# Attention heads of a hybrid decoder layer as one pipeline of branches beside the projection units

## The chip, the cores and the metric

The kernel runs on one core of one Trainium2 chip. The metric is the time of one execution on the device in microseconds (us). The engines are called PE (matmuls; PEld is its weight loading), DVE (vector), ACT (scalar), POOL (GpSimd) and SP (which issues most DMAs). On-chip memory has 128 partitions; matmul results go to eight PSUM buffers, which are handed out here under the tags "g", "s", "t" (two each), "m" and "o" (one each).

## The reference

One layer with 512 tokens and width 2048, all in float32:

```python
h = _rms_norm(x, attn_norm)
proj = h @ w_in     # 8 FoX heads q,k,v + forget gates; 8 NSA heads q; 2 KV groups x (kc,vc,ks,vs,kw,vw); gates
# FoX head:  softmax(q k^T * scale + cum_f[query] - cum_f[key], causal) @ v      (q, k RMS-normed)
# NSA head:  gate0 * compressed + gate1 * selected + gate2 * window attention    (ALiBi slopes, q, k RMS-normed)
#   compressed keys/values: 31 blocks of 32 tokens through cmp_w_k, cmp_w_v
x = x + concat(fox, nsa) @ w_out
h = _rms_norm(x, ffn_norm)
x = x + (silu(h @ w_gate) * (h @ w_up)) @ w_down
```

With 512 tokens the selected branch takes all 8 blocks and the window covers all earlier tokens, so both are causal attention over the full length with their own keys and values.

## The kernel before

Everything is computed transposed, 128 rows of width by 512 tokens. Each float32 operand is split into a high and a low fp32r part (`split`: ACT writes the high part, DVE the low part), and a product is three matmuls (`mm3`: high x high, high x low, low x high).

The work comes in stages. First, `x` and the first weights are loaded and the four token products of kc and vc are formed (`first`). Then come 20 projection *units*: each takes one [2048 x 256] block of `w_in`, in four weight tiles of 1024 columns (`load_w`: a load on SP into one of three "ws" buffers, a split into one of two "wp" buffers), and accumulates 192 matmuls into two "g" buffers (`unit`, `pair_steps`). A unit of queries or keys ends with RMS norms and transposes (`normed`): ACT and DVE square, sum, invert and scale the tile `t` ("tk", one buffer), PE transposes it twice ("nT", four transposes each), and the result is split into a tile of tag "u" (four buffers). A unit of values is split straight into a "u" tile. The second unit carries also the gates (`values_and_gates`, 288 columns).

Beside the units stand the side works. `unload` and `windows` prepare the kc and vc tokens: half 0 goes into the tag "pt" (one buffer, which attention uses for its transposed probabilities), half 1 into "u". `compress` multiplies them with `cmpw` (32 matmuls each for kc and vc, into "m"). `gates` makes gates and forget sums. Then the heads: `nsa(h)` runs the scores of the selected branch (`Branch.scores`: four score tiles, each three matmuls, then DVE adds the bias and takes the row minimum, ACT exponentiates; at the end four DVE multiplies by the inverse sums), the scores of the window branch, the compressed softmax, then the transposes (`Branch.transposes`, ten small PE transposes in three "t" buffers, split into "pt") and the products with the values (`Branch.pv`) of one branch after the other into one "o" buffer. `fox(h)` is one branch, whose bias rows POOL makes from `ckb`, a broadcast load of forget sums. `keep` copies the head's output to its own tile.

All these are Python generators whose steps are interleaved by `weave(main, side, ...)`: for each step of the units, so many steps of the side work. The pairings are written out by hand: two NSA heads beside one unit (nsa_q(2), nsa_q(6)), or beside two (nsa_k(1) with vs1; fox_qk(0) with fox_v(0)); none beside nsa_q(4); two FoX heads beside three units; head 6 beside the last unit; head 7 has no unit beside it. This order is a priority only. The framework plans each engine's queue from it, and puts an instruction whose operands it expects later behind others that it expects to be ready. [...]

After the heads, their outputs are split into the 16 blocks of `bigm` (which held the normalized input until the last unit is done), and 16 output tiles `po` of 48 matmuls with 512 columns follow (`gemm_steps`), each followed by the residual add and the preparation of the feed-forward input (`x1_steps`, `form_sums`, `form_parts`). Then the gate and up stage (`q`, line 971) and the down stage (`pd`) run; the change does not touch them, but for the place of two tiles: `ca` and `cb`, in a pool that takes over the bytes of the weight buffers "ws" and "wp". The load with index 1 of the gate and up stage goes into `cb`, the one with index 4 into `ca`.

Of the kernel before, what the change touches and what calls it, by code (L numbers as in the profile page):

```python
# [16 lines left out]
P = 128  # L17
D = 2048
T = 512
# [34 lines left out]
SHIFT = 8  # L54
SKEW = 48
WSLOT = 2 * HALF * P + P

# [5 lines left out]
UNITS = 2 * NJ  # L63
NOX = 13


@with_exitstack
def hybrid_layer(ctx: ExitStack, tc: tile.TileContext, xT, vec, ffb, wfirst, wgate, win, cmpw, wout, wgu, wdn, out):
# [206 lines left out]
    def pair_steps(name, done):  # L275
# [3 lines left out]
        yield from unit(z, name, win[i], 4, 2 * P, 2 * P, lambda g: done(g, z[g]))  # L279

    def unit_tile(name):
        return ap_.tile([P, 4 * T + 16], FR, tag="u", name=name, bufs=4)

    def normed(na, nb, ga, gb):
# [12 lines left out]
        yield from pair_steps(na, done)  # L297
        nc.vector.tensor_tensor(w, w, e2[:, :, None].to_broadcast([P, NB, 2]), op=OP.add)
        nc.scalar.activation(y, w, AF.Ln, scale=1.0 / HD)
        nc.scalar.activation(y, y, AF.Exp, scale=-0.5)  # L300
        nc.vector.scalar_tensor_tensor(v, w, -0.5 / HD, y, op0=OP.mult, op1=OP.mult)
        nc.vector.tensor_tensor(v, v, y, op=OP.mult)
        nc.vector.scalar_tensor_tensor(y, v, 1.5, y, op0=OP.add, op1=OP.mult)
        nc.vector.tensor_tensor(t, t, y[:, :, :, None].to_broadcast([P, NB, 2, P]), op=OP.mult)
        yield
        r = unit_tile(na)
        for a, (name, gain) in enumerate(((na, ga), (nb, gb))):
            yield
            o = ps.tile([P, T], F32, tag="t", name=f"nT_{name}", bufs=2)
            for i in range(NB):  # L310
                nc.tensor.transpose(o[:, i * P:(i + 1) * P], t[:, i, a, :], ident)
            d = r[:, a * 2 * T:(a + 1) * 2 * T].rearrange("p (s t) -> p s t", s=2)
            split(d, o, gain)
            live[name] = d
            yield

# [10 lines left out]
    def values(na, nb):  # L327
# [9 lines left out]
        yield from pair_steps(na, done)  # L337
        yield

# [13 lines left out]
    class Branch:  # L353
# [5 lines left out]
        def scores(self):  # L359
# [3 lines left out]
            for i in reversed(range(NB)):  # L363
# [6 lines left out]
                nc.scalar.activation(pi, pi, AF.Exp, scale=-1.0, bias=st[:, 0, i:i + 1], accum_out=st[:, 1, i:i + 1])  # L370
                yield
            nc.vector.tensor_scalar_max(st[:, 2], st[:, 1], 1e-30)
# [3 lines left out]
            for i in reversed(range(NB)):  # L376
                pi = p[:, POFF[i]:POFF[i] + P * (i + 1)]
                nc.vector.tensor_scalar_mul(pi, pi, st[:, 2, i:i + 1])

        def transposes(self):  # L380
# [14 lines left out]
        def pv(self, o, start, stop):  # L395
            v, pt = self.v, self.pt
            for n, j in enumerate((0, 1, 3, 2)):
# [7 lines left out]
    def keep(h, o):  # L405
        if h == 0:
            oT[h] = ap_.tile([P, 2, T], F32, tag="fr", name=f"o{h}")[:, 0]
        elif h == NH - 2:
            oT[h] = ap_.tile([P, T], F32, tag="tk", name=f"o{h}")
# [58 lines left out]

    def compressed(h, q, o):
        g = h // 4  # L470
# [26 lines left out]
        yield  # L497
        mm3(o, Vc[:, 0], Vc[:, 1], pt[:64, 0], pt[:64, 1], False, False)
        yield
# [44 lines left out]

    def nsa(h):
        g = h // 4
        q = live.pop(f"qn{h}")
# [4 lines left out]
        o = ps.tile([P, T], F32, tag="o", name=f"on{h}")  # L552
        s, w = [Branch(f"{b}{h}", q, live[f"k{m}{g}"], live[f"v{m}{g}"],
                       lambda i: nb[:, T - P * (i + 1):], 3 * h + c)
                for b, m, c in (("s", "s", 1), ("w", "w", 2))]
        c = compressed(h, q, o)
        yield from s.scores()
        yield from w.scores()
        next(c)
        yield  # L560
        yield from s.transposes()
        next(c)
        yield
        yield from s.pv(o, True, False)
        yield from c
        yield from w.transposes()
        yield from w.pv(o, False, True)
        keep(NH + h, o)

    def fox(h):  # L570
        q, k, v = [live.pop(f"{m}f{h}") for m in "qkv"]
        ck = ap_.tile([P, T], F32, tag="ck", name=f"ckb{h}")
        nc.sync.dma_start(ck, cumd[h:h + 1, :].to_broadcast([P, T]))
        o = ps.tile([P, T], F32, tag="o", name=f"of{h}")

        def nbs(i):
            n = P * (i + 1)
            nb = ap_.tile([P, T], F32, tag="nb", name=f"nbf{h}{i}", bufs=2)
            nc.gpsimd.tensor_scalar(nb[:, :n], ck[:, :n], ncq[:, i, h:h + 1], 1.0, op0=OP.add, op1=OP.mult)  # L579
            nc.gpsimd.affine_select(nb[:, n - P:n], nb[:, n - P:n], pattern=[[-1, P]], compare_op=OP.is_ge,  # L580
                                    fill=BIG, base=0, channel_multiplier=1)
            return nb[:, :n]

        f = Branch(f"f{h}", q, k, v, nbs, None)
        yield from f.scores()
        yield from f.transposes()
        yield from f.pv(o, True, True)
        if h == NH - 1:
            oT[h] = o
        else:  # L590
            keep(h, o)

# [4 lines left out]
    def nsa_q(h):  # L597
        return normed(f"qn{h}", f"qn{h + 1}", gneg[:, 1:2], gneg[:, 1:2])

# [45 lines left out]

    N, NV, NS, FS = 38, 33, 26, 11
    weave(k0, chain(unload(), windows("kc", V_PK)), N, 9, 6)
    weave(values_and_gates("vs0", "vw0"), chain(compress("kc"), windows("vc", V_PV)), 32, 38)
    weave(nsa_q(0), chain(gates(), compress("vc")), N, 35)
    weave(nsa_q(2), chain(nsa(0), nsa(1)), N, 2 * NS)  # L650
    weave(chain(nsa_k(1), values("vs1", "vw1")), chain(nsa(2), nsa(3)), N + NV, 2 * NS)
    run(nsa_q(4))
    weave(nsa_q(6), chain(nsa(4), nsa(5)), N, 2 * NS)
    weave(chain(fox_qk(0), fox_v(0)), chain(nsa(6), nsa(7)), N + NV, 2 * NS)
    for h in range(0, NH - 2, 2):
        weave(chain(fox_qk(h + 1), fox_qk(h + 2), fox_v(h + 2)), chain(fox(h), fox(h + 1)), 2 * N + NV, 2 * FS)
    weave(fox_qk(NH - 1), fox(NH - 2), N, FS)
    last = fox(NH - 1)


    order = list(range(NH, 2 * NH)) + list(range(NH))
    om = []
    for i, h in enumerate(order[:-1]):
        t = big(i)
        split(t, oT[h])
        om.append(t)
    run(last)
    t = big(NK - 1)
    split(t, oT[NH - 1])
    om.append(t)  # L670
    att.close()
# [45 lines left out]

    for m in range(NK):
        n = m // 2 + HALF * (m % 2)
# [494 lines left out]
```

## Time and profile before

| | |
|---|---|
| median of 3 runs | 2147.38 us (2146.97 to 2147.62) |
| the profiled execution | 2147.01 us, its span 2145.3 us |
| granted TensorE clock, mean | 0.997 |
| PE busy | 2113.4 us (99%), 17023 matmuls |
| DVE busy | 1639.2 us (76%) |
| ACT busy | 956.4 us (45%) |
| POOL busy | 185.9 us (9%) |

The span is the time from the first to the last recorded instruction; the execution's own time is 1.7 us longer. Busy times are sums over an engine's instructions. A matmul's end is modelled, and consecutive matmuls overlap in the record, so PE's busy share says little about lost time; the distance from start to start says more. In the lists of waits a line reads: engine, tile and line that waited, the instruction whose result ended the wait, total us, number of waits, longest.

By the tiles' names, the first token products run from about 5 to 50 us, the units with the NSA heads from about 53 to 415, those with the FoX heads to about 710, the output tiles to 872, the gate and up stage and the down stage fill the rest.

### The profile page before, as it was taken

The numbers are of one execution on the slowest core, as the hardware profiler recorded it, in microseconds if no ns is written. First come the engines' busy times: TensorE is split into PE (matmuls) and PEld (weight loads), VectorE is DVE, ScalarE is ACT, GpSimd is POOL, SyncE is SP. The second block draws the span as 40 slices with busy tenths as digits, with TensorE's granted clock in tenths as the row PEclk, the third lists the DMA queues.
The fourth block names the chain that finished last, engine by engine and source line by source line (L and its number), as shares of the span: only waits on it lengthen the run. The fifth ranks groups of instructions, "written<-read, shape, count | busy, mean of one in ns | idle before, by whom it ended". The sixth has DMA issues, their size and how long they took to land.

```text
span 2145.3 us, 40678 instructions
## 1 busy us (share of the span) xinstructions
PE 2113.4 (99%) x17023; PEld 2047.8 (95%) x17023; DVE 1639.2 (76%) x2429; ACT 956.4 (45%) x1179; POOL 185.9 (9%) x297
## 2 busy tenths in 40 slices
PE   8989999999999999999999999999999999999998
PEld 7988999999999888899999999999999999999998
DVE  6656556544445544799999999999999987889898
ACT  5435334433345433443443434333443455565553
POOL 1000000010100000111111111111111000000000
PEclk9999999999999999999999999999999999999999
DMA  5511121132222344567677776777777797579864
GB/s 187 177 65 40 60 70 50 50 99 85 85 89 89 118 147 143 143 186 202 193 182 202 188 197 184 193 201 180 207 186 193 216 341 270 150 230 330 292 180 138
DMA packets 113353, 350.60 MB, mean 163 GB/s; under 512 B 13576, under 2 KB 13576, under 8 KB 113168
## 3 DMA queue, kind: packets, MB, share of 16 engines
q1 hardware_dynamic: 85408, 271.12, 37.6%
q0 software_dynamic: 22144, 52.44, 14.0%
q10 hardware_dynamic: 5616, 24.43, 2.9%
q8 instruction: 133, 2.18, 0.4%
q14 instruction: 52, 0.43, 0.1%
HBM read 319.35 MB, written 74.73 MB: 184 GB/s over the span
## 4 chain that ended last, share of the span: by engine, by line
PE 77%; issue 15%; DVE 3%; POOL 1%; DMA 1%; ACT 1%; ACTq 0%; POOLq 0%; SPq 0%; DVEq 0%
PE q L971 39%; PE pd L1106 13%; PE pd L1111 6%; PE po L149 3%; PE po L148 3%; PE po L147 3%; DMA ckb<-cumd 1%; PE ps_qn L267 1%; PE ps_qn L265 1%; PE ps_qn L268 1%; POOL nbf L579 1%; PE ps_first L149 1%; PE ps_first L147 1%; PE ps_first L148 1%; PE ps_ks L265 1%
## 5 line engine op out<-in xcount | busy, mean ns | idle before, releaser
L79 ACT ACTIVATE bigm<-r 128x1792 fp32r<-128x1792 f32 x174 | 298.2, 1714 | 469.1 <-PE q L971 299.5
L76 DVE TENSOR_TENSOR bigm<-r,bigm 128x1792 fp32r<-128x1792 f32 x174 | 351.5, 2020 | 11.7 <-ACT bigm L79 11.4
L76 DVE TENSOR_TENSOR r<-r 128x512 f32<-128x512 f32 x522 | 267.3, 512 | 28.9 <-DMA r<-wgu 16.8
L971 PE MATMUL q<-formx,bigm 128*128 128x256 f32 x1848 | 218.4, 277 | 2.6 <-ACT bigm L79 2.6
L971 PE MATMUL q<-bigm 128*128 128x256 f32 x1848 | 217.8, 277 | 0.0
L971 PEld LDWEIGHTS q<-formx,bigm 128*128 128x128 f32 x1848 | 214.4, 189 | 2.8 <-ACT bigm L79 2.8
L971 PE MATMUL q<-formy,bigm 128*128 128x256 f32 x1848 | 216.9, 276 | 0.0
L971 PE MATMUL q<-forma,bigm 128*128 128x256 f32 x1848 | 216.8, 276 | 0.0
L971 PEld LDWEIGHTS q<-bigm 128*128 128x128 f32 x1848 | 213.8, 188 | 0.0
L971 PEld LDWEIGHTS q<-forma,bigm 128*128 128x128 f32 x1848 | 213.1, 188 | 0.1
L971 PEld LDWEIGHTS q<-formy,bigm 128*128 128x128 f32 x1848 | 213.0, 188 | 0.1
L121 POOL DMA_DIRECT2D wsum<-wdn x176 | 119.8, 687 | 868.0 <-ACT bigm L79 764.6
L1106 PE MATMUL pd<-bigm 128*128 128x256 f32 x1224 | 147.9, 276 | 0.0
L265 PE MATMUL ps_qf<-wp_qf,bigm 128*128 128x256 f32 x512 | 144.7, 283 | 0.0
L1106 PEld LDWEIGHTS pd<-bigm 128*128 128x128 f32 x1224 | 143.0, 188 | 0.0
L268 PE MATMUL ps_qf<-wp_qf,bigm 128*128 128x256 f32 x512 | 142.7, 279 | 0.0
L267 PE MATMUL ps_qf<-wp_qf,bigm 128*128 128x256 f32 x512 | 142.3, 278 | 0.0
L76 DVE TENSOR_TENSOR bigm<-wd,bigm 128x2048 fp32r<-128x2048 f32 (+1 forms) x64 | 110.3, 1724 | 12.3 <-ACT bigm L79 12.0
L79 ACT ACTIVATE bigm<-rawm 128x768 fp32r<-128x768 f32 (+2 forms) x72 | 65.9, 924 | 109.4 <-PE pd L1111 62.9
L149 PE MATMUL po<-bigm,wp_o 128*128 128x512 f32 x256 | 99.8, 390 | 0.0
L148 PE MATMUL po<-bigm,wp_o 128*128 128x512 f32 x256 | 99.7, 389 | 0.0
L147 PE MATMUL po<-bigm,wp_o 128*128 128x512 f32 x256 | 99.6, 390 | 0.0
(415 smaller groups left out, 4458.0 us busy)
## 6 DMA issues: line engine op xcount, KB each, us to landing
r<-wgu SPq DMA_DIRECT2D x174, 512.0 KB, 4.3
wsum<-wdn POOLq DMA_DIRECT2D x176, 256.0 KB, 4.9
rawm<-ad SPq DMA_DIRECT2D x44, 512.0 KB, 6.5
wd<-wdn SPq DMA_DIRECT2D x40, 512.0 KB, 5.8
wd<-wsum SPq DMA_DIRECT2D x40, 512.0 KB, 6.9
ad<-cb ACTq DMA_DIRECT2D x22, 896.0 KB, 5.6
rawm<-ad SPq DMA_DIRECT2D x44, 384.0 KB, 3.3
ws_qf<-win SPq DMA_DIRECT2D x32, 512.0 KB, 3.2
```

The lines of the kernel that those rows point to most:

```text
L76: return pin(nc.vector.tensor_tensor(*args, op=op))
L79: return pin(nc.scalar.activation(*args, **kw))
L121: d = nc.gpsimd.dma_start(step[0], step[1], **step[2])
L147: nc.tensor.matmul(o, lh, rh, start=start, stop=False)
L148: nc.tensor.matmul(o, lh, rl, start=False, stop=False)
L149: nc.tensor.matmul(o, ll, rh, start=False, stop=stop)
L265: nc.tensor.matmul(o, xg[k][:, 0, c], wp[:, 0, w], start=(k == 0 and b == 0), stop=False, skip_group_check=True)
L267: nc.tensor.matmul(o, xg[k][:, 0, c], wp[:, 1, w], start=False, stop=False, skip_group_check=True)
L268: nc.tensor.matmul(o, xg[k][:, 1, c], wp[:, 0, w], start=False, stop=(k == NK - 1), skip_group_check=True)
L971: nc.tensor.matmul(o, w[wp][:, fb, cs], a[:, xp, fa], start=(k == 0 and h == 0 and wp == 0 and xp == 0), stop=(g == NG - 1 and kk == 1 and ...
L1106: nc.tensor.matmul(b[q][k][:, h * 256:(h + 1) * 256], w[0][:, fb, q * P:(q + 1) * P], a[xp][:, fa], start=(j == 0 and h == 0 and xp == 0), ...
L1111: nc.tensor.matmul(b[q][k][:, h * 256:(h + 1) * 256], w[1][:, fb, q * P:(q + 1) * P], a[0][:, fa], start=False, stop=(j == NJ - 1), skip_g ...
```

## The change

* `weave` now takes a list of side works, each with a first and a last step of the main work between which its steps are spread evenly.
* All units form one stream of 32 steps each (`stream`). A unit of queries or keys leaves its norm's last part behind (`finish`): the elementwise work is issued at the unit's end, the transposes of the two halves after 4 and 6 steps of the next unit.
* All heads form one list of 24 branches (`branches`: selected and window for each NSA head, one for each FoX head). `attend` interleaves the four score steps of a branch with the three transpose steps of the branch before it, and then runs that branch's products. The compressed softmax follows the selected branch's scores, its transposes the window branch's scores, its product stands within the selected branch's products.
* The bias of the next NSA head (`slopes`) and the forget row of the next FoX head (`forget_row`) are made after the first score of a head's first branch.
* 193 steps of attention are spread from step 104 to step 320 (the eight NSA heads; from unit 4 to unit 10 of 20), then 11 at a time over windows of 1.15 to 1.55 units. vc's windows stand at steps 26 to 42 instead of behind kc's products.
* The pool of 13 [128 x 512] buffers becomes 8, and a spare tile of 5 x 512 (tag "x5") that holds one after the other: the first weights in five slices, half 0 of vc's windows, the queries 0 and 1, the queries 4 and 5, the outputs of FoX heads 0 to 4.
* Eight of the 16 output splits stand in the last unit. The first two output tiles are formed together, in the order 8 + 8, 6 + 6, 2 + 2 of their 16 steps, with the last unit's norm and the last head beside them; both residual adds come after.
* Units vs1 and nsa_q(4) change places; `cb` is allocated before `ca`.

No matmul, transpose, elementwise instruction or DMA is added or left out.

```diff
-NOX = 13
+FIN = 4
+NOX = 8
...
-    def weave(main, side, n, m, d=0, r=0):
-        done = 0
-        for i, _ in enumerate(main):
-            while done * (n - d) < (i + 1 - d) * (m - r) and next(side, side) is not side:
-                done += 1
-        run(side)
+    def weave(main, sides, at=0):
+        done = [0] * len(sides)
+        for i, _ in enumerate(main, at + 1):
+            for s, (lo, hi, n, gen) in enumerate(sides):
+                while done[s] < n and i >= lo + (hi - lo) * done[s] / n:
+                    next(gen, None)
+                    done[s] += 1
...
+    def stream(units):
+        behind = iter(())
+        for steps in units:
+            for i, _ in enumerate(steps):
+                if i in (FIN, FIN + 2):
+                    next(behind, None)
+                yield
+            behind = live.pop("finish", iter(()))
+            next(behind, None)
+        live["finish"] = behind
...
             if half == 0:
-                xb = ap_.tile([P, 2, 1280], FR, tag="pt", name=f"xb_{which}").rearrange("p s c -> p (s c)")
+                xb = (ap_.tile([P, 2 * 1280], FR, tag="pt", name=f"xb_{which}") if which == "kc" else spare_unit(f"xb_{which}"))
...
+    def attend(brs):
+        def products(b):
+            if b.start:
+                live["o"] = ps.tile([P, T], F32, tag="o", name=f"o_{b.name}")
+            for n, _ in enumerate(b.pv(live["o"], b.start, b.stop)):
+                yield
+                if n == 0 and b.start and not b.stop:
+                    next(b.side)
+                    yield
+            if b.stop:
+                keep(b.head, live["o"])
+        last = None
+        for b in brs:
+            a = b.scores()
+            t = last.transposes() if last else iter(())
+            for n in range(4):
+                next(a)
+                yield
+                if n == 0:
+                    b.more()
+                if last and n < 3:
+                    next(t)
+                    yield
+            if b.head >= NH:
+                next(b.side)
+                yield
+            if last:
+                yield from products(last)
+            last = b
+        for _ in last.transposes():
+            yield
+        yield from products(last)
...
+    early = spare("early")
     for k in range(NK):
...
-        ws = oxp.tile([P, T], F32, tag="ox", name=f"w0_{k}", bufs=NOX)
+        ws = early[:, k % 5 * T:(k % 5 + 1) * T]
...
+    plan = [(2, 30, 9, chain(unload(), windows("kc", V_PK))), (26, 42, 4, windows("vc", V_PV)),
+            (34, 62, 36, compress("kc")), (66, 96, 40, chain(gates(), compress("vc")))]
+    first_score = 3 * U + FIN + 4
+    plan.append((first_score, 10 * U, 8 * 25 - 7, rest))
+    for a, b in ((10.05, 11.2), (11.25, 12.55), (12.6, 14.15), (14.25, 15.55), (15.6, 17.15), (17.25, 18.55), (18.6, 20)):
+        plan.append((a * U, b * U, 11, rest))
+    plan.append((19 * U + 17, 20 * U, 8, out_splits()))
+    weave(stream(units), plan)
...
+        for k0, k1 in ((0, 8), (8, 14), (14, 16)):
+            for m, n in enumerate((0, HALF)):
+                if k0 % HALF == 0:
+                    wp[m] = load_w(wout[n, k0 // HALF], f"o{n}_{k0 // HALF}")
+                for k in range(k0, k1):
+                    if k == len(om):
+                        out_split()
+                    c = slice(k % HALF * P, (k % HALF + 1) * P)
+                    mm3(z[m], wp[m][:, 0, c], wp[m][:, 1, c], om[k][:, 0, :], om[k][:, 1, :], k == 0, k == NK - 1)
+                    yield
+    plan = [(7, 10, 2, live.pop("finish")), (9, 27, 20, rest)]
+    weave(first_outs(), plan)
+    run(rest)
...
+    cb = fpl.tile([P, 4, T], F32, name="cb")
     ca = fpl.tile([P, 4, T], F32, name="ca")
-    cb = fpl.tile([P, 4, T], F32, name="cb")
```

More of the change, by code (lines that the diff above doesn't have):

```diff
@@ L279, in pair_steps, with spare, spare_unit, normed @@
         yield from unit(z, name, win[i], 4, 2 * P, 2 * P, lambda g: done(g, z[g]))
+    def spare(name, dtype=F32):
+        return oxp.tile([P, 5 * T], dtype, tag="x5", name=name)
+    def spare_unit(name):
+        return spare(name, FR)
     def unit_tile(name):
         return ap_.tile([P, 4 * T + 16], FR, tag="u", name=name, bufs=4)
-    def normed(na, nb, ga, gb):
+    def normed(na, nb, ga, gb, tile=unit_tile):
         t = ap_.tile([P, NB, 2, P], F32, tag="tk", name=f"t_{na}")
@@ L297, in normed @@
         yield from pair_steps(na, done)
[L298 to L304, printed above, removed]
@@ L305, in normed, with finish @@
-        yield
-        r = unit_tile(na)
-        for a, (name, gain) in enumerate(((na, ga), (nb, gb))):
-            yield
[L309 to L315, printed above, removed]
+        def finish():
+            nc.vector.tensor_tensor(w, w, e2[:, :, None].to_broadcast([P, NB, 2]), op=OP.add)
+            nc.scalar.activation(y, w, AF.Ln, scale=1.0 / HD)
+            nc.scalar.activation(y, y, AF.Exp, scale=-0.5)
+            nc.vector.scalar_tensor_tensor(v, w, -0.5 / HD, y, op0=OP.mult, op1=OP.mult)
+            nc.vector.tensor_tensor(v, v, y, op=OP.mult)
+            nc.vector.scalar_tensor_tensor(y, v, 1.5, y, op0=OP.add, op1=OP.mult)
+            nc.vector.tensor_tensor(t, t, y[:, :, :, None].to_broadcast([P, NB, 2, P]), op=OP.mult)
+            yield
+            r = tile(na)
+            for a, (name, gain) in enumerate(((na, ga), (nb, gb))):
+                o = ps.tile([P, T], F32, tag="t", name=f"nT_{name}", bufs=2)
+                for i in range(NB):
+                    nc.tensor.transpose(o[:, i * P:(i + 1) * P], t[:, i, a, :], ident)
+                d = r[:, a * 2 * T:(a + 1) * 2 * T].rearrange("p (s t) -> p s t", s=2)
+                split(d, o, gain)
+                live[name] = d
+                yield
@@ L317, in split_values @@
+        live["finish"] = finish()
+    def stream(units):
[8 more added lines that the diff above has]
+        live["finish"] = behind
     def split_values(r, i, z):
@@ L337, in values @@
         yield from pair_steps(na, done)
-        yield
     def values_and_gates(na, nb):
@@ L395, in pv @@
         def pv(self, o, start, stop):
-            v, pt = self.v, self.pt
+            v, pt = live[self.v], self.pt
             for n, j in enumerate((0, 1, 3, 2)):
@@ L405, in keep @@
     def keep(h, o):
[L406 to L409, printed above, removed]
+        if h == NH - 1:
+            oT[h] = o
+            return
+        if h < NH - 3:
+            if h == 0:
+                live["x5"] = spare("o_fox")
+            oT[h] = live["x5"][:, h * T:(h + 1) * T]
+        elif h < NH - 1:
+            oT[h] = ap_.tile([P, 2 * T], F32, tag=("fr", "tk")[h - NH + 3], name=f"o{h}")[:, :T]
         else:
@@ L467, in compress, with compressed @@
             split(Vc, r)
-    def compressed(h, q, o):
+    def compressed(h, q):
         g = h // 4
@@ L497, in compressed @@
         yield
-        mm3(o, Vc[:, 0], Vc[:, 1], pt[:64, 0], pt[:64, 1], False, False)
+        mm3(live["o"], Vc[:, 0], Vc[:, 1], pt[:64, 0], pt[:64, 1], False, False)
         yield
@@ L543, in gates, with slopes @@
         nc.vector.tensor_scalar_mul(ncq, tq, -1.0)
-    def nsa(h):
-        g = h // 4
-        q = live.pop(f"qn{h}")
+    def slopes(h):
         nb = ap_.tile([P, T], F32, tag="nb", name=f"nb{h}", bufs=2)
@@ L551, in nsa @@
         nc.gpsimd.affine_select(nb, nb, pattern=[[-1, T]], compare_op=OP.is_ge, fill=FAR, base=384, channel_multiplier=1)
[L552 to L591, printed above, removed]
@@ new lines, in slopes, with forget_row, branches, nbs @@
+        live[f"nb{h}"] = nb
+    def forget_row(h):
+        if h < NH:
+            live[f"ck{h}"] = ck = ap_.tile([P, T], F32, tag="ck", name=f"ckb{h}")
+            nc.sync.dma_start(ck, cumd[h:h + 1, :].to_broadcast([P, T]))
+    def branches(first, last):
+        for h in range(first, last):
+            if h < NH:
+                g = h // 4
+                q = live.pop(f"qn{h}")
+                if h == 0:
+                    slopes(0)
+                nb = live.pop(f"nb{h}")
+                for b, c in (("s", 1), ("w", 2)):
+                    br = Branch(f"{b}{h}", q, live[f"k{b}{g}"], f"v{b}{g}", lambda i: nb[:, T - P * (i + 1):], 3 * h + c)
+                    br.head, br.start, br.stop = NH + h, b == "s", b == "w"
+                    br.side = live[f"c{h}"] = compressed(h, q) if b == "s" else live[f"c{h}"]
+                    br.more = (lambda: slopes(h + 1)) if b == "s" and h < NH - 1 else (lambda: None)
+                    yield br
+            else:
+                f = h - NH
+                q, k = live.pop(f"qf{f}"), live.pop(f"kf{f}")
+                if f == 0:
+                    forget_row(0)
+                ck = live.pop(f"ck{f}")
+                def nbs(i):
+                    n = P * (i + 1)
+                    nb = ap_.tile([P, T], F32, tag="nb", name=f"nbf{f}{i}", bufs=2)
+                    nc.gpsimd.tensor_scalar(nb[:, :n], ck[:, :n], ncq[:, i, f:f + 1], 1.0, op0=OP.add, op1=OP.mult)
+                    nc.gpsimd.affine_select(nb[:, n - P:n], nb[:, n - P:n], pattern=[[-1, P]], compare_op=OP.is_ge,
+                                            fill=BIG, base=0, channel_multiplier=1)
+                    return nb[:, :n]
+                br = Branch(f"f{f}", q, k, f"vf{f}", nbs, None)
+                br.head, br.start, br.stop, br.side = f, True, True, iter(())
+                br.more = lambda: forget_row(f + 1)
+                yield br
@@ L644, in unload @@
                 yield
[L646 to L658, printed above, removed]
     order = list(range(NH, 2 * NH)) + list(range(NH))
     om = []
-    for i, h in enumerate(order[:-1]):
-        t = big(i)
-        split(t, oT[h])
+    def out_split():
+        t = big(len(om))
+        split(t, oT[order[len(om)]])
         om.append(t)
-    run(last)
-    t = big(NK - 1)
@@ L669, in hybrid_layer, with out_splits @@
-    split(t, oT[NH - 1])
-    om.append(t)
+    def out_splits():
+        for _ in range(8):
+            out_split()
+            yield
+    U = 32
+    units = [k0, values_and_gates("vs0", "vw0"), nsa_q(0), nsa_q(2), nsa_k(1), nsa_q(4), values("vs1", "vw1"), nsa_q(6),
+             fox_qk(0), fox_v(0)]
+    for h in range(0, NH - 2, 2):
+        units += [fox_qk(h + 1), fox_qk(h + 2), fox_v(h + 2)]
+    units.append(fox_qk(NH - 1))
+    rest = attend(branches(0, 2 * NH))
+    plan = [(2, 30, 9, chain(unload(), windows("kc", V_PK))), (26, 42, 4, windows("vc", V_PV)),
+            (34, 62, 36, compress("kc")), (66, 96, 40, chain(gates(), compress("vc")))]
@@ new lines, in hybrid_layer, with first_outs @@
+    first_score = 3 * U + FIN + 4
[4 more added lines that the diff above has]
+    weave(stream(units), plan)
+    x1steps = {}
+    z = [ps.tile([P, T], F32, tag="g", name=f"po{n}", bufs=2) for n in (0, HALF)]
+    def first_outs():
+        wp = {}
+        for k0, k1 in ((0, 8), (8, 14), (14, 16)):
[4 more added lines that the diff above has]
+                    if k == len(om):
+                        out_split()
+                    c = slice(k % HALF * P, (k % HALF + 1) * P)
+                    mm3(z[m], wp[m][:, 0, c], wp[m][:, 1, c], om[k][:, 0, :], om[k][:, 1, :], k == 0, k == NK - 1)
+                    yield
@@ L716, in x1_steps @@
             tt(acc, acc, sq, op=OP.add)
-    for m in range(NK):
+    for m in range(2):
+        x1s = x1_steps(m)
+        next(x1s)
+        live["z"] = z[m]
+        run(x1s)
+    form_sums(live["raw"])
+    form_parts(0, live["raw"])
+    for m in range(2, NK):
         n = m // 2 + HALF * (m % 2)
```

8 lines of the change are left out of this document (5 added, 3 removed).

## The prediction

> **What bounds the kernel now.** I read the page's busy times first, then the list of who waited for whom on the tensor engine, then the order of time around its longest waits.
>
> ```profile
> span 2145.3 us, 40678 instructions
> PE 2113.4 (99%) x17023; PEld 2047.8 (95%) x17023; DVE 1639.2 (76%) x2429; ACT 956.4 (45%) x1179; POOL 185.9 (9%) x297
> ```
>
> The matmul engine is busy for 99% of the span, so nothing that leaves the number of matmuls alone can bring more than the gaps between them. The change keeps every matmul, transpose, DMA and elementwise instruction and only moves them, so its worth is the waits of PE it removes, less those it makes. From 20 to 720 us (all of the mixer that is touched) PE waited for this:
>
> ```profile
> PE ps_qn L267 <- DVE wp_qn L76: 4.0, 1, 4.0
> PE nT_qf L311 <- DVE t_qf L304: 3.0, 7, 0.7
> PE pcT L494 <- DVE pc L490: 2.2, 6, 0.7
> PE pT_f L390 <- DVE p_f L378: 1.5, 2, 0.9
> PE ps_qn L265 <- ACT vs L319: 1.2, 1, 1.2
> PE pT_s L390 <- DVE pt_s L76: 1.2, 3, 0.5
> PE zkT L464 <- DVE zks L461: 0.5, 1, 0.5
> PE s_s L147 <- DVE st_s L369: 0.5, 2, 0.2
> PE pT_s L390 <- DVE p_s L378: 0.4, 2, 0.2
> PE ps_qn L265 <- DVE tf L349: 0.4, 1, 0.4
> PE nT_qn L311 <- DVE t_qn L304: 0.4, 1, 0.4
> PE nT_ks L311 <- DVE t_ks L304: 0.2, 1, 0.2
> ```
>
> Columns: total us, times, longest us. Together 15.5 us in 28 waits; nearly all end with a vector result. That is idle time as the view counts it, and it is too little, because a matmul's recorded end overlaps the next one's start:
>
> ```profile
> 256.57 0.28 PE L268 MATMUL ps_vs<-wp_vs,bigm 128*128 128x256 f32 x1
> 256.69 0.40 PE L147 MATMUL on<-pt_s,vs 128*128 128x512 f32 x1
> 257.72 0.60 PE L494 MATMUL pcT<-ident,pc 128*64 128x128 f32 x4 [0.64 <-DVE pc L490]
> 258.08 0.48 PE L148 MATMUL on<-pt_s,vs 128*128 128x512 f32 x1
> 258.39 0.39 PE L149 MATMUL on<-pt_s,vs 128*128 128x512 f32 x1
> ```
>
> A matmul of 256 columns is recorded as 0.28 us, yet the next starts 0.12 us later; one of 512 columns takes about twice that, 0.24. Here the next start comes 1.03 us after the one at 256.69, so 0.79 us is lost where the row says 0.64, and the next 512-column matmul takes 0.31 instead of 0.24. I add 0.25 us to each wait: 0.16 hidden, 0.09 to get going again.
>
> **The change part by part.**
>
> (1) The first vc window leaves the one "pt" buffer for the spare tile "x5". Now it cannot be written before the last kc product has read its own window from "pt". These rows show the pile-up that follows, ACT and DVE first, PE after:
>
> ```profile
> 105.23 0.27 ACT L453 ACTIVATE zs_kc<-z_kc 64x128 f32<-64x128 f32 x1 [2.38 <-PE z_kc L450]
> 107.87 0.62 ACT L431 ACTIVATE xb_vc<-xt_vc 128x512 fp32r<-128x512 f32 x1
> 114.12 0.68 DVE L432 TENSOR_TENSOR xb_vc<-xt_vc,xb_vc 128x512 fp32r<-128x512 f32 x1
> 114.88 1.22 DVE L76 TENSOR_TENSOR wp_qn<-ws_qn,wp_qn 128x1024 fp32r<-128x1024 f32 x1
> ```
>
> ```profile
> 108.89 0.29 PE L268 MATMUL ps_fg<-wp_fg,bigm 128*128 128x288 f32 x1
> 110.35 0.36 PE L265 MATMUL ps_qn<-wp_qn,bigm 128*128 128x256 f32 x1 [1.17 <-ACT vs L319]
> 111.85 0.35 PE L265 MATMUL ps_qn<-wp_qn,bigm 128*128 128x256 f32 x1 [0.37 <-DVE tf L349]
> 116.16 0.58 PE L267 MATMUL ps_qn<-wp_qn,bigm 128*128 128x256 f32 x1 [3.95 <-DVE wp_qn L76]
> 116.53 0.41 PE L268 MATMUL ps_qn<-wp_qn,bigm 128*128 128x256 f32 x1
> 119.31 0.41 PE L265 MATMUL ps_qn<-wp_qn,bigm 128*128 128x256 f32 x1
> ```
>
> ```profile
> 113.00:120.00 7.00, 3.85 (x16) 3.45 (x17) 6.44 (x16) 1.60 (x5) 0.61 (x1) 0.51 0.23 75
> 140.00:420.00 280.00, 274.27 (x2091) 257.17 (x2091) 169.03 (x468) 126.09 (x284) 13.52 (x22) 1.00 0.17 54
> 152.00:200.00 48.00, 46.66 (x335) 41.94 (x334) 31.89 (x103) 23.23 (x58) 4.00 (x6) 1.00 0.14 45
> 278.00:303.00 25.00, 24.85 (x216) 24.42 (x215) 8.98 (x13) 6.73 (x10) 0.00 (x0) 1.00 0.28 89
> ```
>
> DVE reaches the second half of the query weights at 114.88, behind four windows and four value evictions, all due within 8 us. From 108.89 up to the one at 119.31 PE starts 17 projection matmuls (14 of them from 116.16 on) and one small transpose. At 0.12 us each these are 2.2 us of 10.4: lost 8.2. Of that, 1.5 us is a halved clock: in the first row (busy us of PE, weight loads, DVE, ACT and POOL with counts, then granted clock, DMA share, GB/s) the granted clock is 0.51, and from 116.53 to 119.31 thirteen starts are 0.214 us apart instead of 0.114 (13 x 0.10 = 1.3, and the first pair). After the change the vc windows come in steps 26 to 42, where the spare tile is free. Their own cover is the gate unit, 32 steps of about 0.8 us. What is late next is the kc normalization chain behind zkT (0.5 us in the list). I take 7.5 us; the ends are 0 (the four value evictions alone keep DVE late) and 8.2.
>
> [...]
>
> (2) Attention as one pipeline, 193 steps spread over 216 unit steps, with the selected branch's transposes and products behind the next branch's scores. The waits that belong to the NSA heads (pcT, pT_s, s_s, nT_qn, nT_ks) are 2.2 + 1.2 + 0.5 + 0.4 + 0.4 + 0.2 = 4.9 us in 15. With 0.25 each: 8.7. Each is a softmax or norm that PE reaches too early. The compressed softmax now gets 3 transposes between it and pcT, after it 11 steps; a score's PSUM buffer gets a transpose and unit work before its next use; norms get 4 unit steps. The vector load, which is 66% in 152 to 200 us and 36% in 278 to 303, where no head runs, evens out to about 60% (169 of 280 us from 140 to 420). Ends: 0 (the vector queue is as late as now) and 14, since waits under 0.15 us are not listed: about 5 more by the same kind of restart. I take 8.7.
>
> (3) Norms and transposes of a projection pair stand in the next unit, and FoX heads use the same pipeline: nT_qf 3.0 in 7 and pT_f 1.5 in 2, with 9 x 0.25: 6.8 us. The last pT_f waits are those of heads 6 and 7, which have only little beside them now; in the new order two output tiles, 32 steps of 3 matmuls or 32 x 3 x 0.24 = 23 us, stand beside the last head. I take 6.8; ends 2 and 7.
>
> (4) The first two output tiles together make one new wait. The last four steps use the second half-matrices of both tiles: tile 0's weight slot comes free when 2 steps of tile 1 (6 x 0.24 = 1.4 us) remain, and must be split for the third tile:
>
> ```profile
> 711.59 1.06 ACT L79 ACTIVATE wp_o<-ws_o 128x1024 fp32r<-128x1024 f32 x1 [1.54 <-PE po L149]
> 712.68 1.23 DVE L76 TENSOR_TENSOR wp_o<-ws_o,wp_o 128x1024 fp32r<-128x1024 f32 x1 [0.40 <-ACT wp_o L79]
> ```
>
> From the release to the end of the second instruction 2.3 us: PE stands about 1 us, 3 at most if the two residual adds go first.
>
> (5) Costed at nothing: five "early" slices plus eight buffers for thirteen shared ones (a load has 5 x 12 x 0.24 = 14 us of matmuls to land, and the row below says 3); the splits of the first eight head outputs in the last unit, hidden by its 192 matmuls (were that cover gone, each would cost PE at most what the larger split in (4) takes, 2.3 us); the forget rows' loads on the SP queue, issued one head ahead as the buffer comes free; head outputs in "x5", free by then.
>
> ```profile
> 1.26 3.09 DMA w<-wfirst
> ```
>
> (6) The swap of ca and cb. These rows show the start of the gate and up stage:
>
> ```profile
> 872.79 0.33 SPq L82 DMA_DIRECT2D cb<-wgu  x1
> 878.57 1.70 ACT L79 ACTIVATE bigm<-cb 128x1792 fp32r<-128x1792 f32 x1 [7.62 <-DVE cb L76]
> 880.32 5.92 PE L971 MATMUL q<-formx,bigm 128*128 128x256 f32 x35 [2.61 <-ACT bigm L79]
> ```
>
> The load into cb is issued only when the last output matmul is done, since cb lies on the second weight slot, and PE then waits 2.6 us. With 0.25 for the restart and, if the clock halves as in (1), another 1.5, that is 4.4 us in all (an estimate). After the swap cb lies on the first slot and on 128 columns of the second. If a load waits for whole tiles, nothing changes; I take that, with 0 and 4.4 as ends.
>
> **Sum.** 7.5 + 8.7 + 6.8 - 1.0 = 22.0 us. The profiled execution took 2147.0 (its span 2145.3 and 1.7 around it), the median of the runs is 2147.4, so the forecast is 2125.
>
> **The rivals.** *The swap pays too.* If only the bytes count, cb loads about 5 us earlier and lands in time: 2125 - 4.4 = 2120.6. For it speaks that the wait is plainly there; against it, that 512 bytes of the live tile are still covered. *The pipeline does nothing*, because the order on each engine is already planned by readiness (output matmuls are pulled ahead of transposes today). Then (2) and the larger part of (3) stay: 2125 + 8.7 + 5 = 2139. *Half of it*: the even load of about 60% on DVE keeps every second wait of (2) and of nT_qf in (3): 4.4 + 2.4 = 6.8, so 2132. *The vector queue decides against it (the other side).* Now all 24 branches are chained: the transposes of a branch follow the next one's first score, and need four multiplies that took this long:
>
> ```profile
> 250.96 1.71 DVE L378 TENSOR_SCALAR p_w<-p_w,st_w 128x512 f32<-128x512 f32 x4
> ```
>
> If weight splits (1.23), next scores and the compressed softmax stand ahead of them, each branch waits. At 1.1 us a branch, 24 x 1.1 = 26 us is more than all that was gained, 22 us plus the 4.3 that a measurement can't tell from no change; at 2 us a branch the kernel takes 2125 + 48 = 2173. Against it: the longest such wait today is 0.9, with less work between. [...]
>
> **How the numbers follow.** Forecast 2125: 0.50, its own range 2118 to 2131. Swap pays: 0.12. Half: 0.15. Pipeline does nothing: 0.10. Vector queue: 0.13, of which 0.07 ends slower by over 0.2% and 0.04 within it. Below 2114 or above 2141 lies less than 2 in 10, so the range is 2114 to 2141. 0.2% or 4.3 us is about what a measurement here can tell from no change: faster 0.89, same 0.04, slower 0.07.
>
> **What would show it.** Right: no half clock near 113 us, xb_vc written before 100 us, no pcT and hardly any nT wait, heads' work on DVE level from 150 to 400 us, the output stage starting some 20 us earlier. Wrong: a new repeated wait of pT on p, PE waiting for wp_o at the third output tile for over 3 us, or a first load issued late; cb still issued after the last po matmul would confirm (6).

## The result, and the profile after

Over four runs the changed kernel takes 2133.95 us (2132.41 to 2136.23), the kernel before beside it 2147.5 us: a ratio of 0.9936 (95% interval 0.9919 to 0.9953), or 13.5 us less. A second series of five runs of the changed kernel gave 2133.92 us and the ratio 0.9936 (0.9924 to 0.9949). The forecast was 2125: faster, as said, but by 60% of what the sum promised.

The page of the changed kernel, its first lines:

```profile
span 2134.5 us, 40677 instructions
PE 2106.5 (99%) x17023; PEld 2047.0 (96%) x17023; DVE 1642.6 (77%) x2429; ACT 956.6 (45%) x1179; POOL 184.2 (9%) x297
```

The work is the same; only its place in time differs. To see where the time went, I cut the span at places that both kernels have. Each row below gives the first and last start of a group of matmuls: the last matmuls of the gate unit, the first ones of the gate and up stage, the last ones of the down stage. First the kernel before, then the changed one:

```profile
L268 PE MATMUL ps_fg<-wp_fg,bigm x64: 292/296/301, 76.0 to 108.9; 128*128 128x288 f32 x64
L971 PE MATMUL q<-forma,bigm x1848: 276/276/281, 872.6 to 1702.8; 128*128 128x256 f32 x185
L1111 PE MATMUL pd<-bigm x612: 276/276/283, 1720.9 to 2138.0; 128*128 128x256 f32 x153
```

```profile
L270 PE MATMUL ps_fg<-wp_fg,bigm x64: 292/296/383, 77.4 to 110.3; 128*128 128x288 f32 x64
L1066 PE MATMUL q<-forma,bigm x1848: 276/276/281, 859.2 to 1692.0; 128*128 128x256 f32 x185
L1206 PE MATMUL pd<-bigm x612: 276/276/283, 1710.1 to 2127.2; 128*128 128x256 f32 x153
```

One more cut is the first matmul of the unit nsa_q(2), from the order in time of PE, before and after:

```profile
149.03 0.28 PE L265 MATMUL ps_qn<-wp_qn,bigm 128*128 128x256 f32 x1
```

```profile
142.54 0.28 PE L267 MATMUL ps_qn<-wp_qn,bigm 128*128 128x256 f32 x1
```

| stretch | before | after | difference | forecast |
|---|---|---|---|---|
| up to the end of the gate unit | 108.9 | 110.3 | +1.4 | 0 |
| the first query unit, to the start of nsa_q(2) | 40.1 | 32.2 | -7.9 | -7.5, step (1) |
| heads, units, output tiles, to the start of gate and up | 723.6 | 716.7 | -6.9 | -14.5, steps (2) to (4) |
| gate and up, down | 1265.4 | 1268.0 | +2.6 | 0, step (6) |

The four differences add to -10.8 us, the difference of the two spans. The first and the last row are not losses that the change makes: in the profile of the second series the gate unit ends at 108.9 and the last row is 1265.7 (857.4 to 2123.1). They vary from run to run; what was measured of the last one is told at the end. What has to be explained is the third row, where half is missing. It can be cut once more, at the first matmul of the third output tile (720.27 before, 706.00 after): up to there, which is steps (2) and (3), the changed kernel takes 7.8 us less (563.5 in place of 571.2) where 15.5 were forecast, and from there to the gate and up stage 0.9 us more (153.2 in place of 152.3), which is step (4), forecast at 1.0. The list of PE's waits in the changed kernel, 20 to 900 us (total us, times, longest):

```profile
PE q L1066 <- ACT bigm L80: 4.6, 1, 4.6
PE nT_qf L320 <- DVE t_qf L314: 2.9, 6, 0.6
PE o_s L149 <- DVE ptc L77: 2.9, 6, 0.7
PE nT_qn L320 <- DVE t_qn L314: 1.1, 3, 0.6
PE pT_s L414 <- DVE pt_s L77: 0.7, 1, 0.7
PE nT_ks L320 <- DVE t_ks L314: 0.6, 1, 0.6
PE po L150 <- DVE wp_o L77: 0.5, 1, 0.5
PE ps_rT L244 <- DVE rstd L200: 0.4, 1, 0.4
```

Gone are the long wait for wp_qn, pcT, pT_f, s_s and most of pT_s. But the norms' transposes (nT) still wait, 4.6 us in 10 where it was 3.6 in 9, and a wait that comes again and again is new: a product of the compressed branch (o_s, line 149) for its own split, 2.9 us in 6. (Two single ones are new as well, ps_rT with 0.4 us and the wp_o of step (4) with 0.5.)

Why the norms still wait is read from the rows behind one unit, whose last matmul starts at 434.37. ACT, then DVE, then PE:

```profile
434.68 0.60 ACT L300 ACTIVATE t_qf<-ps_qf 128x512 f32<-128x512 f32 x1 [2.18 <-PE ps_qf L270]
435.65 1.06 ACT L80 ACTIVATE wp_qf<-ws_qf 128x1024 fp32r<-128x1024 f32 x1
```

```profile
436.75 1.23 DVE L77 TENSOR_TENSOR wp_qf<-ws_qf,wp_qf 128x1024 fp32r<-128x1024 f32 x1
438.49 1.22 DVE L314 TENSOR_TENSOR t_qf<-t_qf,sn_qf 128x1024 f32<-128x1024 f32 x1
```

```profile
438.95 0.28 PE L267 MATMUL ps_qf<-wp_qf,bigm 128*128 128x256 f32 x1
439.77 0.66 PE L320 MATMUL nT_qf<-ident,t_qf 128*128 128x128 f32 x4 [0.54 <-DVE t_qf L314]
```

On both engines a weight split of the next unit (1.06 and 1.23 us) stands inside the norm. From the unit's last matmul to the scaled tile it takes 5.3 us (434.37 to 438.49 + 1.22), and what stands ahead of the transposes on PE does not fill that time. It is more than the four steps written: 34 matmuls of the next unit and six of attention, from 434.48 to about 439.07. The transposes start 0.82 us after the matmul before them, where the 256-column matmuls ahead of them start 0.11 to 0.12 us apart.

The new wait, on DVE and on PE:

```profile
201.22 1.70 DVE L401 TENSOR_SCALAR p_w<-p_w,st_w 128x512 f32<-128x512 f32 x4
202.85 0.68 DVE L77 TENSOR_TENSOR ptc<-pcT,ptc 64x512 fp32r<-64x512 f32 x1
```

```profile
202.37 0.50 PE L148 MATMUL o_s<-ptc,Vc 64*128 64x512 f32 x1
203.58 0.50 PE L149 MATMUL o_s<-ptc,Vc 64*128 64x512 f32 x1 [0.71 <-DVE ptc L77]
```

The transposes of the compressed softmax follow the window branch's last score, so their split is queued behind that branch's four multiplies, and only one product (three matmuls) of the selected branch stands between those transposes and the compressed product. PE can start the high part, not the low one: 1.21 us from start to start, where this kernel's 512-column output matmuls start 0.22 to 0.23 us apart (856.74 to 859.00).

### The profile page after: what moved, and what is told of

It is laid out like the page before. It is cut to its first block, busy times and chain, and to the rows that moved or that the text cites. A ratio compares the mean times of both kernels' runs of the same rounds, so it can differ in the third digit from the quotient of the medians.

```text
span 2134.5 us, 40677 instructions
## 1 busy us (share of the span) xinstructions
PE 2106.5 (99%) x17023; PEld 2047.0 (96%) x17023; DVE 1642.6 (77%) x2429; ACT 956.6 (45%) x1179; POOL 184.2 (9%) x297
## 4 chain that ended last, share of the span: by engine, by line
PE 90%; DVE 5%; ACT 2%; issue 1%; DMA 1%; ACTq 0%; SPq 0%; DVEq 0%
PE q L1066 39%; PE pd L1201 13%; PE pd L1206 6%; PE po L150 3%; PE po L148 3%; PE po L149 3%; PE ps_qf L267 3%; PE ps_qf L270 2%; PE ps_qf L269 2%; PE ps_vf L267 1%; PE ps_vf L270 1%; PE ps_vf L269 1%; PE ps_qn L267 1%; PE ps_qn L270 1%; PE ps_qn L269 1%
## 5 line engine op out<-in xcount | busy, mean ns | idle before, releaser
L77 DVE TENSOR_TENSOR bigm<-r,bigm 128x1792 fp32r<-128x1792 f32 x174 | 351.4, 2020 | 10.8 <-ACT bigm L80 10.2
L77 DVE TENSOR_TENSOR bigm<-wd,bigm 128x2048 fp32r<-128x2048 f32 (+1 forms) x64 | 110.3, 1723 | 11.2 <-ACT bigm L80 10.9
```

What stands on the lines that cost most here:

```text
L77: return pin(nc.vector.tensor_tensor(*args, op=op))
```

## The experiments

Each is timed beside the kernel before (2147.0, 2147.5 and 2148.2 us in the three series). The ratio's 95% interval is in brackets.

| kernel | median us | range | runs | ratio |
|---|---|---|---|---|
| changed, again | 2133.92 | 2132.14 to 2134.66 | 5 | 0.9936 [0.9924, 0.9949] |
| ca before cb again | 2134.66 | 2133.83 to 2135.32 | 5 | 0.9943 [0.9930, 0.9957] |
| cb on the first weight slot alone | 2128.26 | 2127.97 to 2128.56 | 4 | 0.9912 [0.9899, 0.9926] |
| kernel before, with the spare tile only | 2147.57 | 2146.60 to 2150.34 | 11 | 1.0 [0.9991, 1.0009] |
| vc's windows late | 2140.28 | 2136.70 to 2141.57 | 5 | 0.9954 [0.9940, 0.9968] |
| vc's half 0 in "pt", early | 2135.04 | 2132.30 to 2135.22 | 5 | 0.9933 [0.9921, 0.9946] |
| norms later, attention shifted | 2122.50 | 2122.10 to 2124.07 | 4 | 0.9887 [0.9873, 0.9900] |
| attention shifted, norms not | 2128.81 | 2128.03 to 2129.54 | 4 | 0.9911 [0.9898, 0.9925] |
| compressed product later | 2128.62 | 2127.55 to 2131.07 | 4 | 0.9912 [0.9897, 0.9927] |
| together | 2116.46 | 2116.13 to 2116.61 | 4 | 0.9854 [0.9840, 0.9867] |

### The change once more

> The changed kernel once more, as the base of the three others on this chip. 2132 to 2136 us. If the first load into cb lands at very different delays from run to run, its wait at the start of the gate and up stage, 4.6 us in the first profile, comes out different here and moves the time with it.

2133.92 against 2133.95: the size of the gain is settled. The load into `cb` does arrive after different delays. From its issue to the first instruction that reads it, 6.0 us passed in the first profile of the changed kernel and 4.6 in this one (4.1 in the kernel before), and PE's longest wait there was 4.6 and 3.1 us (2.6 before).

### Step (1): the spare tile or the order

With the kernel before and the changed one, three more kernels set two things apart: half 0 of vc's windows in "pt" or in the spare tile, and the windows late (behind kc's products) or early. The first is the kernel before with the spare tile (8 shared buffers; the early weights, half 0 of vc's windows and five FoX outputs in the spare tile, but not the queries), in its old order:

```diff
-NOX = 13
+NOX = 8
-  xb = ap_.tile([P, 2, 1280], FR, tag="pt", ...)
+  xb = (ap_.tile([P, 2 * 1280], FR, tag="pt", ...) if which == "kc" else spare(f"xb_{which}", FR))
```

> The kernel before, with only the first part of the change: 8 buffers and the spare tile x5 for the first weights, vc's first window and FoX outputs 1 to 5; all orders as before. Theory: the 8 us lost at 108 to 119 us come from the one pt buffer alone, since the planner can place the vc windows earlier as soon as they have a tile: no halved clock there, about 2139.5. Rival: the written order (windows behind all kc products) keeps them late; then within 2 us of the kernel before.

It gained nothing. In its order in time the windows stand where they stood, and so does the split behind them:

```profile
113.82 0.68 DVE L439 TENSOR_TENSOR xb_vc<-xt_vc,xb_vc 128x512 fp32r<-128x512 f32 x1
114.58 1.21 DVE L76 TENSOR_TENSOR wp_qn<-ws_qn,wp_qn 128x1024 fp32r<-128x1024 f32 x1
```

The other two start from the changed kernel. One puts the windows back in the old place, the other puts half 0 back into "pt":

```diff
-  (26, 42, 4, windows("vc", V_PV))
+  (59, 65, 4, windows("vc", V_PV))
```

> The changed kernel with vc's windows back behind kc's products (steps 59 to 65 of the units in place of 26 to 42); they still have the spare tile. Theory: the 7.9 us won between the gate unit and the next unit (40.1 us before, 32.2 after) come from the early place, and the spare tile only makes it possible. Then xb_vc is written at about 107 to 114 us again, PE waits some 4 us for wp_qn with a halved clock behind it, and the time is 2134 + 7 = about 2141 us. Rival: in the new plan the rest of the work has moved too, so that a late window finds a free vector queue and the place hardly matters: 2134 to 2136 us.

```diff
-                xb = (ap_.tile([P, 2 * 1280], FR, tag="pt", name=f"xb_{which}") if which == "kc" else spare_unit(f"xb_{which}"))
+                xb = (ap_.tile([P, 2 * 1280], FR, tag="pt", name=f"xb_{which}"))
```

> The changed kernel with half 0 of vc's windows back in the tag pt, at the early place (steps 26 to 42). Theory: the early place needs the spare tile; without it the write of half 0 waits until the last product of kc has read its own window, and the pile-up behind the gate unit returns, perhaps a little larger since the early half's instructions now stand in front of others: 2140 to 2144 us. Rival: half 1 alone (which has its own tile) early is enough, since it takes two of the four windows out of the pile-up: 2134 to 2137 us.

By the medians the late place costs 6.3 us, with the spare tile there. From the end of the gate unit to the start of nsa_q(2) its profile takes 37.5 us, so 5.3 of the 7.9 are gone. One of the four windows was still early in it: the first of the writes below starts at 78.60, the other three at 111.28 and later. The early place keeps the whole gain without the spare tile (32.4 us in that stretch). The writes of the low parts, late in the spare tile, then in the changed kernel:

```profile
L460 DVE TENSOR_TENSOR xb_vc<-xt_vc,xb_vc x4: 625/680/692, 78.6 to 115.3; 128x512 fp32r<-128x512 f32 x4
L460 DVE TENSOR_TENSOR xb_vc<-xt_vc,xb_vc x4: 683/684/686, 67.4 to 81.2; 128x512 fp32r<-128x512 f32 x4
```

Stretches of time around the gate unit's end show it (us, then busy us of PE, weight loads, DVE, ACT, POOL; granted clock, DMA share, GB/s). Early in the spare tile, late in the spare tile, early in "pt":

```profile
112.00:119.00 7.00, 7.00 (x58) 6.33 (x57) 5.54 (x18) 2.61 (x9) 0.66 (x1) 1.00 0.27 94
```

```profile
112.00:119.00 7.00, 4.26 (x32) 3.79 (x31) 6.85 (x22) 2.75 (x7) 0.87 (x1) 0.86 0.09 33
119.00:126.00 7.00, 7.00 (x33) 5.73 (x32) 2.06 (x4) 0.63 (x1) 0.00 (x0) 0.65 0.55 177
```

```profile
112.00:119.00 7.00, 6.87 (x56) 5.98 (x54) 5.53 (x16) 1.96 (x5) 0.66 (x1) 1.00 0.22 75
```

Only the late order fills DVE (6.85 of 7 us) and leaves PE standing (4.26 of 7 us busy), and its granted clock then falls, to 0.65 in the second stretch. Why "pt" did not bind is seen in who waited in the last kernel:

```profile
L460 DVE TENSOR_TENSOR xb_vc<-xt_vc,xb_vc x4: 684/684/693, 79.0 to 93.9; 128x512 fp32r<-128x512 f32 x4
...
  PE z_kc L478: 2.1, 1
```

The write of vc's half 0 waited 2.1 us for a product of kc, once, and was done by 95 us. Both halves were early, not half 1 alone as the rival said: half 0 needs only those products of kc that read its own half, the first 16 of 32. In that kernel the 16th starts at 92.17 and takes 0.37 us; ACT writes the high parts from 92.58 on.

### Steps (2) and (3): norms and the compressed product

First, the transposes of a norm after 8 and 10 steps of the next unit in place of 4 and 6. Attention's start moves with FIN, and three windows of the FoX heads had to move by 0.11 units, so that a head doesn't start ahead of its queries:

```diff
-FIN = 4
+FIN = 8
-  (11.25, 12.55) ... (14.25, 15.55) ... (17.25, 18.55)
+  (11.36, 12.55) ... (14.36, 15.55) ... (17.36, 18.55)
```

> The norm's transposes 8 and 10 steps into the next unit instead of 4 and 6 (three head windows start 0.11 unit later for it). Theory: 4 steps are 0.5 to 0.7 us too short, because the next weight tile's split goes ahead of the norm's small steps on ACT and DVE; the ten nT waits (4.6 us, with 0.25 for each 7 us) go: about 2127. Rival: the order is planned by expected readiness and not by these steps, the waits stay 0.5 us each, and the time is that of the changed kernel.

11.4 us, more than the norms' waits were worth. Its list of waits:

```profile
PE q L1066 <- ACT bigm L80: 2.8, 1, 2.8
PE o_s L149 <- DVE ptc L77: 0.6, 2, 0.4
...
PE pT_s L414 <- DVE p_s L401: 0.3, 1, 0.3
```

The nT rows are gone, but so is most of the row of the compressed product, which this edit did not mean. Two kernels take the parts alone. One shifts attention and the FoX windows in the same way and leaves the norms at 4 steps (`first_score = 3 * U + FIN + 8`):

> The changed kernel with attention begun 4 steps later and the three FoX windows moved as in the late-norm kernel, but the norms still 4 and 6 steps into the next unit. Theory: the gain of the late norms, 11.4 us, is their own; the nT waits stay (4.6 us in 10) and the time is 2132 to 2134.5. Rival: the gain came from the shift of attention against the units; then about 2125 or less.

It lies between the two theories: the shift alone is worth 5.1 us, and the norms' own 4 steps another 6.3 (2128.81 to 2122.50). Its list has

```profile
PE nT_qf L320 <- DVE t_qf L314: 3.3, 6, 0.7
PE o_s L149 <- DVE ptc L77: 1.0, 2, 0.6
...
PE nT_qn L320 <- DVE t_qn L314: 0.5, 2, 0.3
```

so four of the six product waits vanish when attention and units stand against each other otherwise. The other kernel puts the compressed product two products later:

```diff
-                if n == 0 and b.start and not b.stop:
+                if n == 2 and b.start and not b.stop:
```

> The changed kernel with the compressed product two attention steps later among the selected branch's products. Theory: its wait for the split of the compressed probabilities (2.9 us in 6, with 0.25 each 4.4 us) is one step too little between transposes and product: about 2129.5. Rival: the split is late because of the vector queue as a whole and the wait moves to another instruction: 2133 to 2135.

5.3 us, and no o_s row in its list; nT_qf stays at 2.9 in 6, and nT_qn grows from 1.1 to 1.6 in 3.

The medians also hold the varying wait at the start of the gate and up stage, which is told at the end. The stretch from nsa_q(2) to that stage leaves it out: 716.7 and 716.3 us in the two profiles of the changed kernel, 712.8 with the shift alone, 711.9 with the product later, 706.2 with norms later. By it the shift is worth 3.7 us, the norms' own steps 6.6 and the later product 4.6.

The price that the prediction gave a wait, its idle time and 0.25 us, comes near to this. For the product it is 2.9 + 6 x 0.25 = 4.4, less the 0.5 by which nT_qn grew: 3.9 (measured 4.6 by the stretch, 5.3 by the medians). For the norms it is 3.8 in 8 and 0.4 that the product's two waits shrink, 6.2 (measured 6.6 and 6.3).

### Step (6): the place of ca and cb

Undoing the swap:

> ca and cb allocated in the old order, the rest of the change kept. Theory: the swap does nothing, since cb lies on the last weight slot either way; the load is still issued about 0.2 us after the last output matmul, and the time is that of the changed kernel within 1.5 us. Rival: the swap made the load's landing slower (6.0 us against 4.1 before); then this is 2 to 2.5 us faster than the changed kernel.

0.7 us, within what the runs vary by. In this profile the load is issued at 857.31, 0.4 us after the last output matmul starts (856.9), and 5.9 us pass to its first use: neither the late issue nor the slow landing is the new order's. The other kernel adds an unused tile of 256 columns behind `cc`, which moves `cb` so that it lies on the first weight slot alone:

```diff
     cc = fpl.tile([P, 2, T], F32, name="cc")
+    fpl.tile([P, T // 2], F32, name="fill")
```

> An unused tile of 256 columns behind cc moves cb down by 1024 bytes, so that it lies on the first weight slot alone. Theory: the load is issued about 5.5 us earlier (24 matmuls of 0.23 us), PE no longer waits at the second weight block, the clock there is not halved: 4.4 to 7 us faster than the changed kernel, about 2128. Rival: the loads that follow at once delay it wherever it is issued; then less than 1 us.

5.7 us less than the changed kernel, without moving any work. In the changed kernel, then in this one:

```profile
859.42 0.33 SPq L83 DMA_DIRECT2D cb<-wgu  x1
865.46 1.61 DVE L77 TENSOR_TENSOR cb<-cb 128x512 f32<-128x512 f32 x3 [5.58 <-DMA cb<-wgu]
```

```profile
852.31 0.33 SPq L83 DMA_DIRECT2D cb<-wgu  x1
857.87 1.60 DVE L77 TENSOR_TENSOR cb<-cb 128x512 f32<-128x512 f32 x3
```

With 128 columns still on the second slot the load starts 0.42 us after the last output matmul of all (859.00; 859.2 is the first of the next stage). With none it starts 0.42 us after the last one that reads the first slot (851.89, 24 matmuls before the stage's end), and PE does not wait for it.

### Together

Norms later, the product later and the extra tile in one kernel:

> Late norms (8 and 10 steps), late compressed product, and cb on the first weight slot, together. If the three causes are separate: 2122.5 less 5.7 for cb, less what is left of the product's waits (0.6 us in 2, about 1): 2116. If they share their gain, 2118 to 2121.

2116.46 us, 17.5 less than the changed kernel and 31 less than before, the fastest of all. Its list from 20 to 900 us:

```profile
PE po L150 <- DVE wp_o L77: 0.5, 1, 0.5
PE ps_rT L244 <- DVE rstd L200: 0.4, 1, 0.4
PE pT_s L414 <- DVE p_s L401: 0.3, 1, 0.3
PE pcT L522 <- DVE qn L135: 0.2, 1, 0.2
```

The parts do not simply add: by the medians norms later (11.4) and the extra tile (5.7) make 17.1, so the later product brings 0.4 here instead of 5.3; by the stretch from nsa_q(2) it brings 1.5 (704.7 us against 706.2). The shift had already removed nearly all of its waits.

## Why the prediction was right or wrong

(1) was right in size (7.5 forecast, 7.9 between the two profiles) and wrong in cause. It said that vc's windows were late since "pt" was not free. "pt" was free early enough; what kept them late was that they stood behind kc's products in the written order. The buffer's price in the prediction came from reading a pile-up and giving it to the nearest resource that the diff changed. That the plan of each engine is made by readiness pulled no window forward in the kernel before with the spare tile, and one of four in the changed kernel with the late place.

(2) and (3) were the steps that failed. Together they were to give 15.5 and gave 7.8. Two things were wrong. In (3), the seven nT_qf waits were counted as gone because four steps of a unit stand ahead of the transposes, and six are there after the change; I did not set these against the chain on ACT and DVE, 5.3 us with a weight split in the middle of each. With eight steps they are gone. In (2), the three transposes put between the compressed softmax and pcT were enough, and pcT no longer waits; but what comes behind pcT, its split and the product that needs it, got one product of the selected branch in place of all four, and I priced nothing for it. That cost 5.3 us by the medians, 4.6 by the stretch.

The vector-queue rival had the kind of mechanism right (a product waits for a DVE instruction that is queued behind the four multiplies) but put it at the transposes of every branch; it came at the compressed product, six times, 0.5 us each time. The rival "half", at 2132, was nearest in time, though it is not every second wait that stayed: one family left, another stayed whole, and one is new.

By the lists, steps (2) and (3) removed only 3.0 us (9.4 us in 24 waits before, 8.2 in 17 after, with 0.25 for each), where the profiles show 7.8. The rest is in gaps too short for the list, and no run here says which of the moves behind it (the pipeline, the first two output tiles together, the exchanged units) closed them.

(4) was right: 0.5 us of waiting for wp_o, with the restart 0.75, where 1.0 was said; 0.9 is what the stretch from the third output tile lost. (5) was right where it was tried: the kernel with only the spare tile, its eight buffers, its early slices and its FoX outputs stands at 1.0. The output splits in the last unit and the forget rows were not tried alone; the changed kernel's list has no wait for them. (6) was right: the swap does nothing, since in either order the load is issued 0.4 us after the last output matmul starts, and the extra tile shows that the 4.4 us at stake were real, 5.7 even.

Of the signs that the prediction named: no half clock near 113 us, xb_vc done by 82 us, no pcT wait, all seen. "Hardly any nT wait" and the output stage some 20 us earlier were not seen: its first matmul starts 15.6 us earlier (690.44 and 674.86), its third tile 14.3. DVE's work did level out, over 150 to 300 and 300 to 410 us, before and then after (third busy time):

```profile
150.00:300.00 150.00, 146.84 (x1137) 138.24 (x1136) 87.03 (x237) 65.47 (x146) 7.60 (x12) 1.00 0.18 57
300.00:410.00 110.00, 107.43 (x806) 99.61 (x805) 74.88 (x221) 53.11 (x127) 5.92 (x10) 1.00 0.15 49
```

```profile
150.00:300.00 150.00, 145.91 (x1146) 139.92 (x1146) 97.65 (x269) 69.83 (x160) 7.16 (x12) 1.00 0.17 54
300.00:410.00 110.00, 108.87 (x849) 103.95 (x848) 67.86 (x185) 49.74 (x113) 5.74 (x10) 1.00 0.18 58
```

From 58% and 68% to 65% and 62%: a level load on DVE alone did not end PE's waits.

## What to carry to other kernels

When a step is moved away from what feeds it, write down the whole chain that has to fit between (every instruction on every engine, with what is queued ahead of it, here 5.3 us) and set it against the time of the steps put there; then do the same for the next consumer behind the moved one. A late instruction behind a shared buffer may be late by its written place alone: try the place and the buffer separately (here the late place cost 6.3 us by the medians, the shared buffer 1.1). An unused tile that moves a load's target off bytes still in use can be worth as much as a reordering of the work, here 5.7 us for one line.

## What the runs showed of the hardware

The same wait does not cost the same each time. At the start of gate and up, PE waited in the changed kernel's two profiles and in that with norms later for 4.6, 3.1 and 2.8 us; the second profile's row and then 25 us around the wait in these three (the stage starts at 859.2, 857.4 and 847.6):

```profile
PE q L1066 <- ACT bigm L80: 3.7, 3, 3.1
```

```profile
855.00:880.00 25.00, 20.44 (x139) 19.50 (x138) 17.48 (x22) 9.54 (x7) 1.87 (x4) 0.86 0.46 146
```

```profile
855.00:880.00 25.00, 21.19 (x166) 19.96 (x164) 18.76 (x23) 10.34 (x8) 2.37 (x4) 1.00 0.54 179
```

```profile
843.60:868.60 25.00, 22.24 (x161) 21.34 (x160) 19.07 (x24) 10.04 (x8) 2.36 (x4) 0.93 0.50 165
```

Taken by the microsecond, the granted clock in the first profile of the changed kernel is 0.50 in each from 867 to 873, 0.92 in the one before and 0.67 in the one behind, and 1.00 around them: 6.8 us at half speed, worked out from these shares. In the kernel before, where the wait is 2.6 us, it is 0.60, 0.50, 0.50 and 0.70 from 881 to 885 and 1.00 around: 3.4 us. By the same reckoning 0.93 over 25 us is 3.5 us at half speed (an estimate) and 1.00 none: after 3.1 us of waiting none, after 2.8 us 3.5. Two other profiles have the same wait of 4.0 us there, and the clock over such a stretch is 0.93 in one (product later, 849 to 874) and 0.86 in the other (the kernel before with the spare tile, 868 to 893). So the length of the wait alone doesn't decide; what else does, no run here shows.

From the start of gate and up to the last matmuls of the down stage it takes 1265.4 to 1267.0 us in the five profiles at 1.00 or 0.93, 1267.7 to 1268.7 in the five at 0.86, and 1261.3 in both with the extra tile, where the wait is gone. The two profiles of the changed kernel are 4.1 us apart: 2.3 lie in this stretch, 1.4 ahead of the gate unit's end, for which no run shows a cause. With the extra tile alone the four runs spread over 0.6 us.
